# A two-layer hybrid decoder trunk on one core: the opening in a fixed order, the first mixer's order and memory, and the norms' partition sums in two passes

## The chip, the cores and the metric

The kernel runs on 1 core of one Trainium2 chip. Times are microseconds (us) of device time. The times of the kernel before are three runs on one chip. The profile is one further execution, recorded by the hardware profiler.

## What is computed

Two layers over 1024 tokens of width 1024. In each layer the token mixer's width is split into four groups of 256 (short gated convolution, sparse attention, gated linear attention, chunked gMLP) that are fed by one input projection, normalised group by group and joined by one output projection; a squared-ReLU MLP of width 4096 follows. Both halves stand between RMS norms whose scale, shift and gate come from `cond @ w_mod`.

```python
def reference(x, c, ...):
    cond = jax.nn.silu(c)
    for l in range(DEPTH):
        mod = cond @ w_mod[l] + b_mod[l]
        sh1, sc1, gt1, sh2, sc2, gt2 = [m[:, None, :] for m in jnp.split(mod, N_MOD, axis=-1)]
        h = rms_norm(x, norm_g[l, 0]) * (1.0 + sc1) + sh1
        y = mixer_block(h, positions, w_in[l], ..., w_o[l])
        x = x + gt1 * rms_norm(y, norm_g[l, 1])
        h = rms_norm(x, norm_g[l, 2]) * (1.0 + sc2) + sh2
        y = jnp.square(jax.nn.relu(h @ w_up[l])) @ w_down[l]
        x = x + gt2 * rms_norm(y, norm_g[l, 3])
    return x
```

## The kernel before

Activations lie with the width on the partitions: a tile is 128 features by 512 tokens, and `hf` counts the two halves of 512 tokens. The stages are start(), mix(0,0), mix(0,1), ff(0,0), mix(1,0), ff(0,1), mix(1,1), ff(1,0), ff(1,1), where the first number is the layer and the second `hf`. A scheduler reorders the instructions of all stages and gives each engine one stream, which runs in order; the order in which the code is written and priorities (`tc.high_priority`, `LATER`) steer it.

**Matmuls.** Each fp32 operand is split into a high part in fp32r and the rest. `mm3` does a product in three fp32r matmuls (L173 high by high, L174 high by low, L175 low by high). `wunit` brings four 128x128 blocks of weights: a 256 KB load on SyncE's queue (L158), a cast on ScalarE (L167), a subtraction on VectorE (L131). Twelve matmuls belong to a unit, two units to an output tile (`gemm`). Loads go through rings of raw buffers (`raw_a` 3, `raw_b` 3, `raw_f` 5) and split buffers (`w_a` 4, `w_b` 4, `w_f` 6, two per unit). mix(0,0) takes its projection weights through lane "b", its output projection through lane "a"; the MLP takes lane "f".

**Norms.** `rms_R` squares eight (or two) tiles on ScalarE, adds them on VectorE, sums over partitions by one fp32 matmul with a matrix of ones (L195) and takes the inverse root by a logarithm and an exponential (L199, L200). 33 norms are done: 31 over 512 tokens, 2 (the last) over 256. `make_h` scales and shifts the tiles and splits them into `h` (L140, L209).

**Modulation.** A column of `w_mod` is summed against `cond` by a VectorE instruction with an accumulator: in start() 1024 wide (`mod_dot`, L239, tiles `mw`), later in two halves of 512 (`mod_half`, L247), whose 256 KB loads go through `raw_b` in mix(0,0) and through `raw_f` in the MLPs.

**start().** It builds the rotary tables, reads x and six blocks of `w_in` (`EARLY`), does the columns of shift and scale one k at a time, and makes `h` k by k; with each k go 18 matmuls into six PSUM banks, 144 in all. The scheduler orders all of it. x of half 1 is loaded behind it.

**mix(0,0).** Gates, attention (`nsa_part`; its steps transpose probabilities, cast and subtract them, and multiply them with the values: L777, L779, L782, L783), GLA (`gla_part`, a loop over four chunk pairs that starts at L592), gMLP and convolution, then the 24 columns of gate 1, shift 2 and scale 2 in 48 halves (`mods_now`), the attention's group norm, the split of all eight group tiles, and the output projection (`yo`, L946). `between` does the first norm of half 1 there.

**Ends of the mixers.** After the output projection come a norm, the residual with a reload of x (`xo`) and a second norm (`h2`); `LATER` lowers their priority by 800 in all mixers but the first. ff(1,0)'s last down-projection group adds into tiles `yf` of a region of its own.

## Time and profile before

| | us |
|---|---|
| median of 3 runs (lowest, highest) | 2635.78 (2635.64, 2638.55) |
| the profiled execution | 2634.88 |
| its span | 2633.1 |
| TensorE (PE) busy | 2488.4 (95%) |
| VectorE (DVE) busy | 1631.0 (62%) |
| ScalarE (ACT) busy | 1310.5 (50%) |
| mean DMA rate | 116 GB/s |

Busy time of a matmul overlaps that of the next one, so the distance from one start to the next is what a matmul costs in a full stream. In a list of waits a row names the waiting engine, the tile that it writes and its line, then what it waited for, with the time in total, the number of waits and the longest. In the time order each row has start, duration, engine, line, operation, output and inputs, shape and count (rows of neighbours of one kind are joined); in brackets stands the idle time ahead of it on its engine and what ended it.

### The profile page before, as it was taken

What the parts mean: (1) busy time and instruction counts of PE and PEld (TensorE: products, weight loads), DVE (VectorE), ACT (ScalarE), POOL (GpSimd) and SP (SyncE); (2) the same over time, 40 slices, a digit from 0 to 9 for tenths busy, and PEclk for the clock granted to TensorE, in tenths of its full rate; (3) what the DMA queues carried; (4) which work ended last, traced back from release to release, by engine and by line L of the source; (5) the groups of instructions that cost most, each with busy time, mean ns of one, the idle gap of its engine ahead of it and who ended that gap; (6) DMA issues with size and microseconds to landing.
All of it is one profiled execution on the core that took longest, in us unless ns stands there. A gap on an engine that the chain in (4) does not pass through costs nothing.

```text
span 2633.1 us, 34406 instructions
## 1 busy us (share of the span) xinstructions
PE 2488.4 (95%) x11834; PEld 1987.3 (75%) x11834; DVE 1631.0 (62%) x3425; ACT 1310.5 (50%) x2657; POOL 53.0 (2%) x65
## 2 busy tenths in 40 slices
PE   5899499999999999999999999999999998899997
PEld 3666277777877878887787878877788876788886
DVE  7676866557888577444676476544567755634445
ACT  3573345445665356344366445444466744443333
POOL 0100000000000000000100000000100000000000
PEclk9899699999999999999999999999999999999999
DMA  8313634345434454322522344322322134433332
GB/s 279 100 46 100 203 117 132 106 140 153 129 123 134 155 164 140 102 85 89 154 83 70 116 152 140 99 84 79 119 77 68 57 108 143 136 97 96 97 97 75
DMA packets 176200, 305.79 MB, mean 116 GB/s; under 512 B 21573, under 2 KB 33434, under 8 KB 176026
## 3 DMA queue, kind: packets, MB, share of 16 engines
q1 hardware_dynamic: 176026, 303.60, 36.7%
q8 instruction: 93, 1.52, 0.2%
q14 instruction: 81, 0.66, 0.1%
HBM read 281.50 MB, written 17.83 MB: 114 GB/s over the span
## 4 chain that ended last, share of the span: by engine, by line
PE 83%; DVE 6%; DMA 4%; issue 1%; ACT 1%; POOL 0%; DVEq 0%; SPq 0%; ACTq 0%; POOLq 0%
PE ps_ff L173 16%; PE ps_ff L174 16%; PE ps_ff L175 16%; PE ps_mm L173 8%; PE ps_mm L175 8%; PE ps_mm L174 8%; DMA raw_f<-in_w_mod_dram 2%; PE ps_pv L783 1%; PE ps_mm L777 1%; PE ps_pv L782 1%; PE ps_s L822 1%; DMA raw_b<-in_w_mod_dram 1%; PE ps_s L824 1%; PE ps_t L777 1%; PE ps_t L195 1%
## 5 line engine op out<-in xcount | busy, mean ns | idle before, releaser
L167 ACT CAST w_f<-raw_f 128x512 fp32r<-128x512 f32 x504 | 311.7, 619 | 426.3 <-PE ps_ff L174 409.2
L131 DVE TENSOR_TENSOR w_f<-raw_f,w_f 128x512 fp32r<-128x512 f32 x504 | 350.4, 696 | 178.7 <-ACT w_f L167 167.9
L173 PE MATMUL ps_ff<-hid,w_f 128*128 128x512 f32 x992 | 395.4, 399 | 21.7 <-DVE yf L137 12.7
L175 PE MATMUL ps_ff<-h,w_f 128*128 128x512 f32 x1024 | 405.4, 396 | 1.2 <-DVE w_f L131 1.2
L173 PE MATMUL ps_ff<-h,w_f 128*128 128x512 f32 x1024 | 403.1, 394 | 0.0
L174 PE MATMUL ps_ff<-h,w_f 128*128 128x512 f32 x1024 | 402.3, 393 | 0.0
L174 PE MATMUL ps_ff<-hid,w_f 128*128 128x512 f32 x992 | 392.4, 396 | 1.5 <-DVE hid L131 1.5
L175 PE MATMUL ps_ff<-hid,w_f 128*128 128x512 f32 x992 | 391.7, 395 | 0.0
L173 PE MATMUL ps_mm<-h,w_a 128*128 128x512 f32 x784 | 318.2, 406 | 32.6 <-ACT yo L946 23.7
L175 PE MATMUL ps_mm<-h,w_a 128*128 128x512 f32 x784 | 317.2, 405 | 6.0 <-DVE w_a L131 6.0
L174 PE MATMUL ps_mm<-h,w_a 128*128 128x512 f32 x784 | 314.8, 403 | 3.6 <-DVE h L131 3.6
L167 ACT CAST w_a<-raw_a 128x512 fp32r<-128x512 f32 x196 | 121.3, 620 | 304.5 <-PE ps_mm L174 278.7
L131 DVE TENSOR_TENSOR w_a<-raw_a,w_a 128x512 fp32r<-128x512 f32 x196 | 135.1, 689 | 179.2 <-ACT w_a L167 173.3
L173 PEld LDWEIGHTS ps_ff<-hid,w_f 128*128 128x128 f32 x992 | 188.1, 190 | 69.8 <-DVE yf L137 15.2
L175 PEld LDWEIGHTS ps_ff<-h,w_f 128*128 128x128 f32 x1024 | 192.3, 188 | 45.5 <-issue 2.9
L173 PEld LDWEIGHTS ps_ff<-h,w_f 128*128 128x128 f32 x1024 | 192.4, 188 | 43.0 <-issue 3.1
L174 PEld LDWEIGHTS ps_ff<-h,w_f 128*128 128x128 f32 x1024 | 192.4, 188 | 42.0 <-issue 2.2
L174 PEld LDWEIGHTS ps_ff<-hid,w_f 128*128 128x128 f32 x992 | 188.3, 190 | 44.6 <-issue 2.9
L175 PEld LDWEIGHTS ps_ff<-hid,w_f 128*128 128x128 f32 x992 | 187.9, 189 | 41.1 <-issue 1.4
L137 DVE TENSOR_TENSOR y<-y,ps_ff 128x512 f32<-128x512 f32 (+1 forms) x208 | 138.0, 664 | 125.0 <-PE ps_ff L175 123.8
L173 PEld LDWEIGHTS ps_mm<-h,w_a 128*128 128x128 f32 x784 | 149.9, 191 | 72.8 <-ACT yo L946 24.1
L175 PEld LDWEIGHTS ps_mm<-h,w_a 128*128 128x128 f32 x784 | 149.8, 191 | 44.5 <-DVE w_a L131 7.7
(390 smaller groups left out, 3610.2 us busy)
## 6 DMA issues: line engine op xcount, KB each, us to landing
raw_f<-in_w_up_dram SPq DMA_DIRECT2D x256, 256.0 KB, 2.7
raw_f<-in_w_down_dram SPq DMA_DIRECT2D x256, 256.0 KB, 2.7
raw_a<-in_w_in_dram SPq DMA_DIRECT2D x132, 256.0 KB, 2.6
raw_f<-in_w_mod_dram SPq DMA_DIRECT2D x112, 256.0 KB, 2.9
raw_a<-in_w_o_dram SPq DMA_DIRECT2D x64, 256.0 KB, 2.7
raw_b<-in_w_mod_dram SPq DMA_DIRECT2D x48, 256.0 KB, 3.1
mw<-in_w_mod_dram SPq DMA_DIRECT2D x16, 512.0 KB, 5.7
bp<-in_cmp_w_dram SPq DMA_DIRECT2D x32, 256.0 KB, 5.7
```

The source lines that it names most:

```text
L131: V.tensor_tensor(out=out, in0=a, in1=b, op=ALU.subtract)
L137: eng.tensor_tensor(out=out, in0=a, in1=b, op=ALU.add)
L167: A.copy(hi, raw)
L173: PE.matmul(ps_ap, wh, xh, start=start, stop=False)
L174: PE.matmul(ps_ap, wh, xl, start=False, stop=False)
L175: PE.matmul(ps_ap, wl, xh, start=False, stop=stop)
L195: PE.matmul(p, ones, acc, start=True, stop=True)
L777: PE.transpose(tp[0:kn, hh, :], cols(h0 + hh), ident)
L782: PE.matmul(pv[:, h0:h0 + nh, :], vst, th[0:kn], start=first[0], stop=False)
L783: PE.matmul(pv[:, h0:h0 + nh, :], vst, tl[0:kn], start=False, stop=last)
L822: PE.matmul(sp[:, 0:w], qh[:, h0 + hh, :], KX[:, 128 * k0:128 * k0 + w], start=True, stop=False)
L824: PE.matmul(sp[:, 0:w], ql[:, h0 + hh, :], KX[:, 128 * k0:128 * k0 + w], start=False, stop=True)
```

## The change

Three things are changed, and two small ones with them.

1. start() is written in a fixed order (`tc.manual_schedule()`). The small loads (gains, biases, frequencies, positions, selection matrix) and the stores of the rotary tables go to GpSimd's queue. The order of the large loads is c, x, the first two `mw`, six weight blocks, four `mw`, and so on, with six `mw` tiles instead of four. The rotary tables are a generator whose pieces stand between the k steps. `h` is made by a VectorE multiplication with R, a ScalarE scaling and shift, and `split` (ScalarE cast, VectorE subtraction). x of half 1 is loaded in `between`.
2. In mix(0,0) a generator, `beside["b"]`, does one of the 24 modulation columns behind each lane-"b" weight unit until all are done. The attention's group norm is written right behind attention; groups are split one by one; all regions of memory are open at once, with GLA's tiles in the ring of x tiles ("y", 8) and in the pool of `h`. The output projection does the second half of the width (GLA and attention) of six outputs into six PSUM banks first, then the first half, then two whole outputs.
3. In `rms_R` the accumulated squares are cast to fp32r on ScalarE, the rest is taken on VectorE, and two fp32r matmuls with ones replace the fp32 one.
4. `LATER` of mix(1,1) is 0 instead of 800.
5. In ff(1,0) `yf` and `xo` lie in the pool of `h` (`spare`).

```diff
-LATER = {(0, 0): 0, (0, 1): 800, (1, 0): 800, (1, 1): 800}
+LATER = {(0, 0): 0, (0, 1): 800, (1, 0): 800, (1, 1): 0}
...
         for n in names:
-            dma(out=par[l][n], in_=src[n][l])
+            P.dma_start(out=par[l][n], in_=src[n][l])
...
             hi, lo = wunit(lane, src[:, 4 * kh:4 * kh + 4, :], [128, 4, 128])
+            if lane in beside:
+                next(beside[lane], None)
...
+    def gemm_part(ps_ap, lane, src, h, kh, start, stop):
+        hi, lo = wunit(lane, src[:, 4 * kh:4 * kh + 4, :], [128, 4, 128])
+        for k in range(4):
+            mm3(ps_ap, hi[:, k, :], lo[:, k, :], h[4 * kh + k][0], h[4 * kh + k][1],
+                start and k == 0, stop and k == 3)
...
         with tc.high_priority(offset=400):
-            PE.matmul(p, ones, acc, start=True, stop=True)
+            hi, lo = (work.tile([128, T], F32R, name="nt", tag="nt", bufs=3)[:, cs] for _ in range(2))
+            A.copy(hi, acc)
+            sub(lo, acc, hi.bitcast(F32))
+            PE.matmul(p, ones_r, hi, start=True, stop=False)
+            PE.matmul(p, ones_r, lo, start=False, stop=True)
...
+        with region("kw", "right") as kw, region("rp") as rp, region("su") as su, tc.manual_schedule():
...
             for k in range(8):
...
+                msum(k, ms[k])
+                if k == 0:
+                    next(tables)
+                if k < 5:
+                    ms.append(mload(k + 3))
+                if k == 2:
+                    raws = wload(1)
+                mul(xt[k], xt[k], R)
                 if k % 4 == 0:
-                    raws = [wload(n, k // 4) for n in EARLY]
-                hs += make_h(xt, R, d["A1"], d["mod"][:, 0, :], (k,))
...
+                    wsplit(raws)
+                t = nt()
+                A.activation(t, xt[k], AF.Identity, scale=d["A1"][:, k:k + 1], bias=d["mod"][:, 0, k:k + 1])
+                hs.append(split(t))
...
+                next(tables, None)
...
         for j in js:
             for k in range(8):
                 mod_half(l, j, k, lambda src, shape: wraw(lane, src, shape))
-            mod_scale(l, j, slice(0, 8))
+                if k == 7:
+                    mod_scale(l, j, slice(0, 8))
+                yield
...
+                with region("wb", "right") as lane_pool["b"], region("gl", "right") as rg, \
+                        region("cv", "right") as rgc, region("gm", "right") as rgm:
+                    beside["b"] = mods_now(0, (2, 4, 3), "b")
+                    gates, lrT = gate_part(l, hf, h, gr, rg, "a", early)
+                    yn = nsa_part(l, hf, h, es.enter_context(region("ns")), gates, early)
+                    on = [split(t) for t in group_out(yn, "t", gain[:, 2:4])]
+                    ol = [split(t) for t in gla_part(l, hf, h, rg, "b", sx, lrT)]
+                    og = [split(t) for t in gmlp_part(l, hf, h, rgm, "b", sx)]
+                    oc = [split(t) for t in conv_part(l, hf, h, rgc, "b", sx)]
+                    for _ in beside.pop("b"):
+                        pass
...
+            if opening:
+                for o in range(6):
+                    sums[o] = ps(("mm", "mm", "ff", "ff", "s", "s")[o])
+                    gemm_part(sums[o], "a", w_o[l, o], outs, 1, True, False)
             for o in range(8):
-                p = ps("mm")
-                gemm(p, "a", w_o[l, o], outs, (6, 7, 4, 5, 2, 3, 0, 1) if opening else range(8))
+                if o in sums:
+                    p = sums[o]
+                    gemm_part(p, "a", w_o[l, o], outs, 0, False, True)
+                else:
+                    p = ps("mm")
+                    gemm(p, "a", w_o[l, o], outs, range(8))
...
-            down(NGRP - 1, yo=lambda: rg.tile([128, T], F32, name="yf", tag="yf", bufs=8))
+            down(NGRP - 1, yo=(lambda: rg.tile([128, T], F32, name="yf", tag="yf", bufs=8)) if l == 0 else spare)
...
-    xt = load_x(1)
-    h = mix(0, 0, h, lambda: norm(0, 1, xt), early)
+    h = mix(0, 0, h, lambda: norm(0, 1, load_x(1)), early)
```

Lines move by 2 to 60: L131, L173 to L175, L195, L239, L247, L777, L782 and L592 of before are L133, L177 to L179, L210 with L211, L255, L263, L827, L832 and L642 of after.

VectorE in the opening, before, in the middle of the k steps. `ISA mw` is the sum of a 1024-wide column, `ISA ma` its read-out:

```order
L239 ISA mw,ma<-mw,cond 128x1024
L239 ISA ma 128x1
L137 TENSOR_TENSOR mod_100<-ma,bmod_97 128x2
L140 SCALAR_TENSOR_TENSOR nt<-y,A_101,nt 128x512
L239 ISA mw,ma<-mw,cond 128x1024
L239 ISA ma 128x1
L140 SCALAR_TENSOR_TENSOR h<-nt,mod_100,h 128x512
L140 SCALAR_TENSOR_TENSOR A_101<-mod_100,ng_96 128x1
L239 ISA mw,ma<-mw,cond 128x1024
```

The same place after, one k step and the start of the next:

```order
L255 ISA mw,ma<-mw,cond 128x1024
L255 ISA ma 128x1
L255 ISA mw,ma<-mw,cond 128x1024
L255 ISA ma 128x1
L139 TENSOR_TENSOR mod_102<-ma,bmod_99 128x2
L142 SCALAR_TENSOR_TENSOR A_103<-mod_102,ng_98 128x1
L136 TENSOR_TENSOR y<-y,nt 128x512
L133 TENSOR_TENSOR h<-nt,h 128x512
L255 ISA mw,ma<-mw,cond 128x1024
```

The sums of the next columns stood between the two steps of an `h`; now they stand behind its subtraction.

SyncE's queue in the first mixer, before (`raw_b` from w_in is a projection weight, `qh` and `ql` are attention's queries):

```order
L767 DMA qh<-qh 64x2x128 x2
L767 DMA ql<-ql 64x2x128 x2
L158 DMA raw_b<-in_w_in_dram 128x512 x5
L767 DMA qh<-qh 64x2x128 x2
L767 DMA ql<-ql 64x2x128 x2
L158 DMA raw_b<-in_w_in_dram 128x512 x11
```

The same after:

```order
L817 DMA qh<-qh 64x2x128 x2
L817 DMA ql<-ql 64x2x128 x2
L160 DMA raw_b<-in_w_in_dram 128x512
L160 DMA raw_b<-in_w_mod_dram 128x512 x2
L160 DMA raw_b<-in_w_in_dram 128x512
L160 DMA raw_b<-in_w_mod_dram 128x512 x2
L160 DMA raw_b<-in_w_in_dram 128x512
L160 DMA raw_b<-in_w_mod_dram 128x512 x2
```

Weights stood in a row; now two halves of a modulation column stand between any two.

TensorE at the end of attention in the first mixer, before (`ps_mm<-h,w_b` are projections of the mixer):

```order
L175 MATMUL ps_mm<-h,w_b 128x512
L783 MATMUL ps_pv<-w_a,VW 128x512
L777 MATMUL ps_t<-ident,bp 128x128 x4
L455 MATMUL ps_ff<-wsT,xm 64x128 x16
L782 MATMUL ps_pv<-w_a,VW 128x512
L783 MATMUL ps_pv<-w_a,VW 128x512
L777 MATMUL ps_t<-ident,bp 128x128 x4
L173 MATMUL ps_mm<-h,w_b 128x512
```

After, the end of attention, the attention's norm and the start of the GLA loop:

```order
L827 MATMUL ps_t<-ident,bp 128x128 x4
L832 MATMUL ps_pv<-w_a,VW 128x512
L833 MATMUL ps_pv<-w_a,VW 128x512
L827 MATMUL ps_t<-ident,p 32x128 x4
L832 MATMUL ps_pv<-w_a,VC 128x512
L833 MATMUL ps_pv<-w_a,VC 128x512
L210 MATMUL ps_t<-nt,ones_r 128x512
L211 MATMUL ps_t<-nt,ones_r 128x512
L642 MATMUL ps_ff<-gh,g 128x512
L652 MATMUL ps_ff<-gh,g 64x128 x2
```

Projections stood between attention's steps until the end; now none stands between the last twelve steps, the norm and the GLA loop, and the gMLP's and convolution's last 14 units (168 matmuls) stand behind them.

## Rows read from the trace of the kernel before

**Rows 1.** waits of TensorE over the whole run

```profile
PE ps_mm L173 <- ACT yo L946: 23.7, 1, 23.7
...
PE ps_ff L173 <- DVE yf L137: 12.7, 3, 12.1
...
PE ps_mm L173 <- ACT h L222: 7.0, 1, 7.0
...
PE ps_mm L174 <- DVE h L131: 3.6, 1, 3.6
```

**Rows 2.** stretches: length, busy us (count) by engine, granted clock, DMA share, GB/s

```profile
25.00:50.00 25.00, 12.04 (x36) 8.16 (x37) 21.94 (x46) 6.36 (x11) 0.00 (x0) 1.00 0.96 342
...
250.00:275.00 25.00, 10.26 (x32) 5.75 (x30) 21.64 (x60) 9.46 (x17) 0.00 (x0) 0.69 0.64 200
...
275.00:300.00 25.00, 15.47 (x50) 11.29 (x50) 21.57 (x59) 8.39 (x14) 0.64 (x1) 0.77 0.65 203
...
300.00:325.00 25.00, 5.71 (x15) 4.56 (x16) 21.28 (x56) 8.02 (x13) 0.00 (x0) 0.52 0.71 230
```

**Rows 3.** time order of TensorE around a norm's matmul

```profile
292.25 1.02 PE L195 MATMUL ps_t<-nt,ones 128*128 128x512 f32 x2
292.86 0.65 PE L175 MATMUL ps_mm<-h,w_a 128*128 128x512 f32 x1
293.34 0.39 PE L173 MATMUL ps_mm<-h,w_a 128*128 128x512 f32 x1
```

**Rows 4.** group of VectorE up to 82 us; time order of TensorE

```profile
L239 DVE CUSTOM_DVE_ANT_0 mw<-mw,cond 128x1024 f32<-128x1024 f32 x16 | 19.3, 1220 | 1.0 <-DMA mw<-in_w_mod_dram 0.9
...
40.00 1.22 PE L173 MATMUL ps_mm<-h,w_k 128*128 128x512 f32 x2 [11.59 <-ACT h L209]
...
74.76 0.39 PE L175 MATMUL ps_s<-h,w_k 128*128 128x512 f32 x1
...
102.57 0.77 PE L173 MATMUL ps_mm<-h,w_b 128*128 128x512 f32 x1
```

**Rows 5.** SyncE's queue at 108 us; DMA landings; groups of 100:250 and 249:322

```profile
108.25 15.25 SPq L158 DMA_DIRECT2D raw_b<-in_w_in_dram  x5
...
raw_b<-in_w_in_dram SPq DMA_DIRECT2D x11, 256.0 KB, 2.6
...
raw_b<-in_w_mod_dram SPq DMA_DIRECT2D x48, 256.0 KB, 3.1
...
L167 ACT CAST w_b<-raw_b 128x512 fp32r<-128x512 f32 x29 | 17.9, 618 | 24.1 <-PE ps_mm L174 18.6 <-issue 4.4 <-ACT bp L832 1.0
...
L131 DVE TENSOR_TENSOR w_b<-raw_b,w_b 128x512 fp32r<-128x512 f32 x29 | 19.9, 687 | 13.8 <-ACT w_b L167 13.8
...
L247 DVE CUSTOM_DVE_ANT_0 raw_b<-raw_b,cond 128x512 f32<-128x512 f32 x48 | 32.9, 687 | 6.8 <-DMA raw_b<-in_w_mod_dram 6.7
```

**Rows 6.** time order of TensorE, two attention steps

```profile
196.25 0.60 PE L777 MATMUL ps_t<-ident,bp 128*128 128x128 f32 x4
...
198.85 1.05 PE L777 MATMUL ps_t<-ident,bp 128*128 128x128 f32 x4
```

**Rows 7.** time order of TensorE, two starts of the GLA loop

```profile
180.42 1.08 PE L592 MATMUL ps_ff<-g 128*128 128x512 f32 x2
...
185.02 1.08 PE L592 MATMUL ps_ff<-g 128*128 128x512 f32 x2
```

**Rows 8.** time order of TensorE around the output projection's stop

```profile
295.20 0.40 PE L175 MATMUL ps_mm<-h,w_a 128*128 128x512 f32 x1
...
319.29 0.80 PE L173 MATMUL ps_mm<-h,w_a 128*128 128x512 f32 x1 [23.70 <-ACT yo L946]
```

**Rows 9.** time order of TensorE and VectorE at mix(1,1)'s end

```profile
2230.92 2.08 PE L195 MATMUL ps_t<-nt,ones 128*128 128x512 f32 x2 [5.15 <-DVE nt L137]
...
2244.35 1.28 DVE L137 TENSOR_TENSOR yf<-y,ps_ff 128x512 f32<-128x512 f32 x2
...
2245.08 0.79 PE L173 MATMUL ps_ff<-hid,w_f 128*128 128x512 f32 x1 [12.08 <-DVE yf L137]
```

More of the change, by code (lines that the diff above doesn't have):

```diff
@@ L83, in trunk_kernel @@
                     fill=0.0, base=0, channel_multiplier=-1)
+    ones_r = const.tile([128, 128], F32R, name="ones_r")
+    A.copy(ones_r, ones)
     V.memset(bones, 0.0)
@@ L201, in rstd, with make_h @@
         return R
-    def make_h(xt, R, Ac, shc, ks=range(8)):
+    def make_h(xt, R, Ac, shc):
         h = []
-        for k in ks:
+        for k in range(8):
             t = nt()
@@ L266, in start @@
         d = par[0]
-        early = {}
-        rope_tables()
-        with region("kw", "right") as kw, region("su") as su:
-            def mk(src, shape):
-                t = su.tile(shape, F32, name="mw", tag="mw", bufs=4)
-                dma(out=t, in_=src)
-                return t
-            def wload(n, kh):
-                raw = kw.tile([128, 4, 128], F32, name="raw_k", tag="raw_k", bufs=6)
-                dma(out=raw, in_=w_in[0, n, :, 4 * kh:4 * kh + 4, :])
-                return raw
-            def wsplit(raw):
-                hi, lo = (kw.tile([128, 4, 128], F32R, name="w_k", tag="w_k", bufs=12) for _ in range(2))
-                A.copy(hi, raw)
-                sub(lo, raw, hi.bitcast(F32))
-                return hi, lo
+        early, hs, ws = {}, [], {}
@@ new lines, in start, with wload, wsplit, mload @@
+        load_params(0, ("ng", "bmod"))
+        with region("kw", "right") as kw, region("rp") as rp, region("su") as su, tc.manual_schedule():
+            def wload(kh):
+                raws = []
+                for n in EARLY:
+                    raw = kw.tile([128, 4, 128], F32, name="raw_k", tag="raw_k", bufs=6)
+                    dma(out=raw, in_=w_in[0, n, :, 4 * kh:4 * kh + 4, :])
+                    raws.append(raw)
+                return raws
+            def wsplit(raws):
+                for n, raw in zip(EARLY, raws):
+                    hi, lo = (kw.tile([128, 4, 128], F32R, name="w_k", tag="w_k", bufs=12) for _ in range(2))
+                    A.copy(hi, raw)
+                    sub(lo, raw, hi.bitcast(F32))
+                    ws[n] = hi, lo
+            def mload(k):
+                ts = [su.tile([128, 1024], F32, name="mw", tag="mw", bufs=6) for _ in range(2)]
+                for j in (0, 1):
+                    dma(out=ts[j], in_=w_mod[0, 8 * j + k])
+                return ts
+            bm = d["bmod"].rearrange("p (j k) -> p j k", k=8)
+            def msum(k, ts):
+                ma = work.tile([128, 2, 1], F32, name="ma", tag="ma", bufs=4)
+                for j in (0, 1):
+                    mod_dot(0, j, k, lambda src, shape: ts[j], ma[:, j, :])
+                add(d["mod"][:, 0:2, k:k + 1], ma, bm[:, 0:2, k:k + 1])
+                mod_scale(0, 1, slice(k, k + 1))
@@ L286, in start @@
             for hf in range(2):
-                t1, t2 = (su.tile([128, T], F32, name="ct", tag="ct", bufs=4) for _ in range(2))
                 ch = cond[:, hf * T:hf * T + T]
                 dma(out=ch, in_=c[:, hf * T:hf * T + T].to_broadcast([128, T]))
+            xt = load_x(0)
+            tables = rope_tables(rp)
+            for hf in range(2):
+                t1, t2 = otile(), otile()
+                ch = cond[:, hf * T:hf * T + T]
                 logsig(t2, ch, t1)
@@ L337, in trunk_kernel, with rope_tables @@
     sind = dram.tile([2, 128, T], F32, name="sind")
-    def rope_tables():
-        with region("rp") as rp:
+    def rope_tables(rp):
+        if True:
             def tk(n):
@@ L485, in gla_part, with ht @@
         d = par[l]
+        opening = (l, hf) == (0, 0)
         def gt(shape=(128, T)):
+            if opening:
+                return work.tile(list(shape), F32, name="g", tag="y", bufs=8)
             return rg.tile(list(shape), F32, name="g", tag="g", bufs=10)
+        def ht(shape):
+            return hp.tile(list(shape), F32, name="gh", tag="h", bufs=32) if opening else gt(shape)
         def inproj(k):
@@ L935, in mix @@
                 yn = nsa_part(l, hf, h, es.enter_context(region("ns")), gates)
-            on = group_out(yn, "t", gain[:, 2:4])
-            outs = [split(t) for t in oc + og + ol + on]
+                on = group_out(yn, "t", gain[:, 2:4])
+                oc, og, ol, on = ([split(t) for t in g] for g in (oc, og, ol, on))
+            outs = oc + og + ol + on
         res = None
@@ L1054, in load_x @@
             t = ytile()
-            dma(out=t, in_=xT[hf, :, k, :])
+            load(out=t, in_=xT[hf, :, k, :])
             xt.append(t)
```

48 lines of the change are left out of this document (18 added, 30 removed).

## The prediction

> **What bounds the kernel now.** I read the waits of TensorE over the whole run first. The engine is busy 95% of the 2633.1 us span, so some 145 us of idle time are all that an order can win, and a saving elsewhere counts only where TensorE itself is short of time. The waits say where the idle time lies [rows 1]: one of 23.7 us on the copy of an output tile, 7.0 and 3.6 us on the first split tiles of the output projection, and 12.1 us (of 12.7) on the last sums of ff(1,0)'s down projection. The table by stretches puts them on the clock [rows 2]: from 250 to 325 us TensorE works 10.26, 15.47 and 5.71 of 25 us each, 43.6 us lost, at granted clocks of 0.69, 0.77 and 0.52. That is the tail of the first mixer: the 48 modulation columns, two 256 KB loads' worth of VectorE sums each pair, sit in front of the output projection's copies there. Last I read the matmuls of the norms and the stretch in which attention and the gated linear attention (GLA) run.
>
> The profiled run took 2634.88 us (span 2633.1); the median of the runs shown is 2635.78, so a sum made on the trace gets 0.9 added.
>
> **Part 1, the norms' sums.** One fp32 matmul against ones shows as two records that together hold the engine 0.86 us at full clock: the records start at 292.25, the next at 292.86 and the one after at 293.34, of which one ordinary 0.23 us step belongs to the matmul between [rows 3]. Two fp32r passes are two ordinary steps, 0.46. The saving is 0.40 us for each of 31 norms of 512 columns. About 26 lie where TensorE is the bound: 26 x 0.40 = 10.5 us less. Five (opening, mixer's groups, the norm before ff) lie in idle time and save nothing. Each norm also gains a ScalarE cast and a VectorE subtraction before its matmul, 0.62 + 0.69 us by the same operations on a weight unit of equal size [rows 5], so 1.3 us on the chain of a norm that is waited for. Where up-projection matmuls stand behind, that is hidden; in the very last norm nothing stands behind it: +1.1 net. Bounds for this part: -13 (all 31) to -6 (ten of the norms find their matmuls waited for by what follows).
>
> **Part 2, the opening.** Before, VectorE does for each k two sums of 1024 columns (1.22 us each, some 1.15 from start to start) and the two steps of an `h` (an estimated 0.75 each), 3.8 in all, and the first of the 144 early matmuls starts at 40.00, the last starts at 74.76 and is through at 75.3 [rows 4]: from 40 on TensorE sets the pace, 18 matmuls x 0.23 = 4.1 us per k. After, the k step is written in a fixed order: sums, multiply, then ScalarE's scaling and cast, then the subtraction, and the next k's sums stand behind that subtraction on VectorE. Per k: 2.3 + 0.15 + 0.69 + (some 0.7 + 0.62, waited for) + 0.69 + hand-overs, some 5.4 us, now above TensorE's 4.1. The start is earlier, since x and the first w_mod are no longer behind the six weight loads and the second half of x is not loaded here: by my chain (condition ready near 12, eight squares, taken at a cast's 0.62, to 18, first sums 21.6, table operations 4.5, multiply, six weight subtractions x 0.69 [rows 5], subtraction; the 12 and the 4.5 are estimates) the first h is there near 32.5. At k = 4 six weight casts and the table's copy stand in front on ScalarE, and that copy waits for TensorE to finish k = 3: about 5 us more. 32.5 + 7 x 5.4 + 5 + 4.1 = 79.4, against 75.3: +4, between -3 (per k 4.4) and +10 (first h at 38).
>
> **Part 3, the first mixer.** This decides. Gone are the three waits of 23.7, 7.0 and 3.6 us and most of the rest of the 43.6. Three things come instead.
> First, the weight ring. Three raw buffers now take weight, column, column in turn, so each weight has always the same buffer and its load is issued only when the previous weight has been cast and subtracted. Load 2.6 to 3.1, cast 0.62, subtraction 0.69 [rows 5] make 3.9 to 4.4 us; with the two 0.69 us sums and attention's work in VectorE's queue I take 4.5. Before, five weight loads went out in 15.25 us, 3.05 each. TensorE needs 2.75 per unit (12 matmuls). Eighteen units stand before the end of the interleaved part; from a first one near 107 (before 102.57 [rows 4], plus the opening's 4) they last to 107 + 81 = 188, and the attention pieces put among them bring some 6 more: 194.
> Second, with no projection matmul among them, twelve attention steps, the attention's group norm, the GLA loop and its norms now follow one another. A step that runs alone takes 2.6 us, 196.25 to 198.85 [rows 6]; the GLA loop 4.6 per step, 180.42 to 185.02 [rows 7], with other work between. 12 x 2.6 + 9 (norm chain: squares, add, cast, subtraction, logarithm, exponential, two gains, splits) + 4 x 4.6 + 8.5 = 67 (the 9 and the 8.5 are estimates from the durations of such operations), ends 261; before, projections filled this time (29 units are cast between 100 and 250 us [rows 5]).
> Third, fourteen units remain: two stand ready (2.75 each), four still alternate with columns (4.5), eight run at 2.75: 45 us. SyncE's queue has seven loads of the second half of x in the middle of them, 1.8 MB that at 342 GB/s [rows 2] take 5.4 us, with the following weights queued behind; they need the GLA tiles free, which they are by then. Conv ends at 261 + 45 + 5.4 = 311.5, and 16 output units x 2.75 = 44 bring 355; the conv norm hides under the first halves of six outputs (16.5 us), so that no split is waited for. I add 3 for the clock when TensorE comes out of the stretch at half speed, as the granted 0.77 and 0.52 around the restarts show here [rows 2]: 358.
> Before: 295.20 is the last matmul of the second output, and the remaining 144 run from 319.29 [rows 8], 144 x 0.23 + 2 for the low clock, to 354.4. The part is worth +3.5 with the opening in it. Bounds: -10 (attention 2.2, GLA 3.6 per step when VectorE is free, ring 4.2) to +22 (ring 5.5). I stay in the middle because each step has a row.
>
> **Part 4, the end of mix(1,1).** The lowered priority goes, and 60 up-projection matmuls instead of 93 stand behind the residual's norms. Before, the second norm's matmul starts at 2230.92 after 5.15 idle, and the last sums only at 2244.35, in VectorE's queue behind the scaled tiles; TensorE restarts at 2245.08 [rows 9]. After, the norm comes some 5 us earlier and 1.3 later, cover is 33 x 0.23 = 7.6 shorter, but these 33 matmuls still have to be done later: their time is not lost. The sums go to spare tiles, and still stand behind the scaled tiles. I take 0, from -5 to +5.
>
> **Sum.** 2634.88 - 10.5 + 1.1 + 3.5 + 0 = 2629.0, plus 0.9: **2630 us**.
>
> **The rivals.**
> *Ring slower (slower than before).* Each load of a column or weight is waited for in order, and VectorE's queue holds attention's subtractions behind a sum whose load has not landed. At 5.6 us per unit the 18 units cost 18 x 1.1 = 20 us: 2650. It decides from 5.1 per unit on (11 us more than forecast, 2641). For it: the trace before already loses 6.7 us of 73 in VectorE sums waiting for loads [rows 5], and attention's DMAs share the queue. Against: loads are two at a time, with 67 us of slack only afterwards. 0.22.
> *Serial stretch shorter.* If steps alone take 2.2 and GLA 3.6, with VectorE no longer casting weights between, 4.8 + 4 us go, and 3 more in the norms: 2618. 0.18.
> *Opening at half clock.* TensorE would work 4.1 of every 5.4 us. In 275 to 300 it worked 15.47 of 25 and was granted 0.77 [rows 2]; at the low level of the two (1.2 against 2.4 GHz) the 0.23 us step becomes up to 0.46, so 18 take up to 8.2 us, more than VectorE's 5.4. Eight of those, 66, from 32.5 end at 98, 19 later than forecast: 2649. Against it: from 25 to 50 us the engine was busy 12.04 of 25 and was granted 1.00 [rows 2]. 0.06. The Trainium skill (TensorE: Matmul & The Clock Gate, HAM oscillation) has a kernel whose bursts of matmuls between waits fell back to the half rate every time; by it this rival would be the forecast.
> *Norms win nothing.* If what follows a norm waits for its longer chain, the 10.5 go: 2640. 0.08.
>
> **How the numbers follow.** The forecast has 0.46, with a range of its own of 2618 to 2641. About 0.2% (5.3 us) is what a measurement of this kernel tells from no change: 2630.5 to 2641.1. Of the forecast's 0.46, 0.27 lies below that and 0.19 in it. Faster: 0.27 + 0.18 = 0.45; same: 0.19 + 0.08 = 0.27; slower: 0.22 + 0.06 = 0.28. The range reaches from the shorter stretch's lower side, 2610, to a little past the ring's 2650: 2653.
>
> **What will show it.** The first early matmul near 32 us and the last near 79; weight loads of the first mixer 4.5 us apart; between about 194 and 261 us no projection matmul and a granted clock near half; no wait of 20 us on an output copy; the output projection done near 358; the norm's two matmuls 0.46 us together. It is wrong if projections start again before 250 or after 275, or if the time up to the second mixer moves by over 15 us.

## The result, and the profile after

| | before | after |
|---|---|---|
| median, us (lowest, highest) | 2635.71 (2633.18, 2638.55) | 2681.78 (2677.83, 2684.12) |
| span of the profiled execution | 2633.1 | 2682.1 |
| TensorE idle, summed over its waits | 133.1 | 164.3 |

The ratio is 1.0173 [1.0155, 1.0191]: the change makes the kernel 46 us slower. The forecast was 2630, and the upper end of its range 2653.

The two spans are 49 us apart. Where these come from is read by putting the same matmul of both traces side by side, counted from the start of its kind:

| matmul | before | after | shift |
|---|---|---|---|
| first of the 144 early ones | 40.00 | 29.75 | -10.2 |
| last of the 144 | 74.76 | 100.55 | +25.8 |
| first with lane "b" weights (`w_b`) | 102.57 | 133.09 | +30.5 |
| last of the 18th unit | 207.94 | 211.22 | +3.3 |
| last with `w_b` | 255.76 | 357.11 | +101 |
| last of the output projection | 355.22 | 401.82 | +46.6 |
| second norm behind the first mixer (L195, L210) | 388.49 | 435.85 | +47.4 |
| last norm in front of mix(1,1)'s end | 1872.14 | 1914.04 | +41.9 |
| end of the span | 2633.1 | 2682.1 | +49.0 |

So nearly everything is lost in the first 402 us: 26 us in the opening, partly regained by units that go early, then far more in the first mixer.

TensorE's waits over the whole run (in total, times, longest), against [rows 1]: the largest are now on norms and on the `h` of the opening, and none is on an output tile `yo`. The 18.4 us are the time ahead of TensorE's first instruction.

```profile
PE ps_t L210 <- ACT nt L208: 36.2, 4, 18.4
...
PE ps_mm L177 <- ACT h L238: 25.9, 8, 9.8
```

**The opening.** TensorE's rows of after, in order of time, are these. Line L177 is `mm3`'s first matmul (L173 before), L417 the transposes of the table's piece, L423 its selection:

```profile
29.75 0.80 PE L177 MATMUL ps_mm<-h,w_k 128*128 128x512 f32 x1 [9.85 <-ACT h L238]
...
41.67 0.49 PE L177 MATMUL ps_mm<-h,w_k 128*128 128x512 f32 x1 [2.03 <-ACT h L238]
...
46.48 1.12 PE L423 MATMUL ps_pv<-nt,sl 17*128 17x512 f32 x2
49.63 0.49 PE L177 MATMUL ps_mm<-h,w_k 128*128 128x512 f32 x1 [2.04 <-ACT h L238]
...
80.05 0.79 PE L177 MATMUL ps_mm<-h,w_k 128*128 128x512 f32 x1 [2.04 <-ACT h L238]
...
87.21 1.12 PE L423 MATMUL ps_pv<-nt,sl 17*128 17x512 f32 x2
...
90.37 0.50 PE L177 MATMUL ps_mm<-h,w_k 128*128 128x512 f32 x1 [2.04 <-ACT h L238]
```

The k steps start 8.0 us apart (41.67, 49.63) and 10.3 us apart later (80.05, 90.37). The later one is longer because its 18 matmuls take 7.2 us (80.05 to 87.21), where the granted clock is 0.60 (80.00 to 87.30), against 4.8 us (41.67 to 46.48) at 1.00 (41.60 to 46.50). ScalarE's rows at the same place:

```profile
39.68 0.57 ACT L419 COPY nt<-ps_t 17x512 f32<-17x512 f32 x1 [9.98 <-PE ps_t L417]
40.16 0.81 ACT L343 ACTIVATE nt<-y,mod,A 128x512 f32<-128x512 f32 x1
41.00 0.62 ACT L238 CAST h<-nt 128x512 fp32r<-128x512 f32 x1
47.63 0.59 ACT L425 COPY of<-ps_pv 128x512 f32<-128x512 f32 x1 [6.02 <-PE ps_pv L423]
```

ScalarE sits idle for 9.98 and 6.02 us in front of a copy whose matmul stands behind all 18 of step k. Behind that copy in its queue stand the scaling and the cast that make `h` of step k+1. So TensorE cannot start k+1 until it has ended k, its own table piece, a copy, a scaling and a cast: at full clock that is 4.8 us from 41.67 to 46.48 (18 x 0.23 and the wait for the low half of `h`) and 3.2 from there to 49.63. Six of the seven steps have such a copy.

**The first mixer.** Windows of after (start:end, its length, busy time and count of PE, PEld, DVE, ACT and POOL, granted clock, DMA share, GB/s), to be held against [rows 2]:

```profile
25.00:50.00 25.00, 14.03 (x43) 9.53 (x43) 14.64 (x38) 5.25 (x8) 0.57 (x1) 1.00 0.44 143
50.00:75.00 25.00, 17.36 (x54) 12.16 (x54) 15.03 (x30) 6.94 (x12) 0.54 (x1) 0.81 0.42 150
75.00:100.00 25.00, 19.75 (x63) 13.11 (x62) 9.73 (x22) 6.87 (x11) 1.49 (x3) 0.85 0.37 126
...
225.00:250.00 25.00, 17.98 (x47) 10.36 (x47) 8.85 (x23) 6.72 (x18) 0.00 (x0) 0.50 0.10 37
250.00:275.00 25.00, 12.67 (x30) 5.57 (x30) 11.07 (x28) 7.93 (x17) 1.27 (x2) 0.50 0.12 38
275.00:300.00 25.00, 17.65 (x56) 9.37 (x56) 4.75 (x18) 6.79 (x18) 1.90 (x3) 0.50 0.10 32
300.00:325.00 25.00, 16.73 (x83) 13.21 (x84) 17.64 (x33) 10.81 (x21) 0.00 (x0) 0.71 0.26 85
```

From 225 to 300 the count of matmuls is small, VectorE, ScalarE and GpSimd are idle most of the time, DMA moves 32 to 38 GB/s, and the clock is at its lower level throughout. TensorE's rows of that stretch show what runs there: attention steps (L827), the attention's norm (L210), the GLA loop (L642), and the first projection at the end:

```profile
211.22 0.40 PE L179 MATMUL ps_mm<-h,w_b 128*128 128x512 f32 x1
...
212.85 0.60 PE L827 MATMUL ps_t<-ident,bp 128*128 128x128 f32 x4
...
239.20 1.05 PE L827 MATMUL ps_t<-ident,bp 128*128 128x128 f32 x4
...
242.24 1.05 PE L827 MATMUL ps_t<-ident,bp 128*128 128x128 f32 x4
...
259.33 0.79 PE L210 MATMUL ps_t<-nt,ones_r 128*128 128x512 f32 x1 [4.73 <-ACT nt L208]
...
266.06 2.04 PE L642 MATMUL ps_ff<-gh,g 128*128 128x512 f32 x2 [5.21 <-DVE gh L638]
...
272.96 2.02 PE L642 MATMUL ps_ff<-gh,g 128*128 128x512 f32 x2
...
279.84 2.02 PE L642 MATMUL ps_ff<-gh,g 128*128 128x512 f32 x2
...
309.20 0.78 PE L177 MATMUL ps_mm<-h,w_b 128*128 128x512 f32 x1
```

No projection matmul runs from 211.22 to 309.20, 98 us. Yet two units were split and ready long before 309: VectorE's last subtractions for `w_b` lie at 213.58 and 220.18, and the next projection matmul stands in TensorE's stream behind the whole chain.

```profile
213.58 0.69 DVE L133 TENSOR_TENSOR w_b<-raw_b,w_b 128x512 fp32r<-128x512 f32 x1
...
220.18 0.69 DVE L133 TENSOR_TENSOR w_b<-raw_b,w_b 128x512 fp32r<-128x512 f32 x1
```

The loads of the weights in the interleaved part are issued 5.30 us apart here, with two halves of a column behind each; over all 18 units the pace is (211.22 - 133.09) / 18 = 4.34 us.

```profile
203.56 0.33 SPq L160 DMA_DIRECT2D raw_b<-in_w_in_dram  x1
204.17 1.85 SPq L160 DMA_DIRECT2D raw_b<-in_w_mod_dram  x2
208.86 0.33 SPq L160 DMA_DIRECT2D raw_b<-in_w_in_dram  x1
```

TensorE hardly waits for them. The window of the 18 units (columns as above), and all of TensorE's waits in it, 1.5 us together:

```profile
133.00:211.30 78.30, 76.70 (x413) 60.82 (x412) 65.39 (x217) 49.21 (x129) 0.00 (x0) 0.95 0.52 159
...
PE ps_pv L833 <- DVE w_a L133: 1.2, 1, 1.2
PE ps_mm L179 <- DVE w_b L133: 0.3, 1, 0.3
```

**The norms, and the end of mix(1,1).** Two norm matmuls of after (L210, L211) stand among projections, each 0.23 from the next start, against [rows 3]:

```profile
326.81 0.39 PE L210 MATMUL ps_ff<-nt,ones_r 128*128 128x512 f32 x1
327.04 0.40 PE L177 MATMUL ps_mm<-h,w_b 128*128 128x512 f32 x1
...
327.51 0.39 PE L211 MATMUL ps_ff<-nt,ones_r 128*128 128x512 f32 x1
327.74 0.40 PE L179 MATMUL ps_mm<-h,w_b 128*128 128x512 f32 x1
```

At the end of mix(1,1) the waits of TensorE, against [rows 9], are 10.64 and 13.63 where they were 5.15 and 12.08:

```profile
2277.38 0.80 PE L210 MATMUL ps_t<-nt,ones_r 128*128 128x512 f32 x1 [10.64 <-ACT nt L208]
2292.53 0.80 PE L177 MATMUL ps_ff<-hid,w_f 128*128 128x512 f32 x1 [13.63 <-DVE sp L139]
```

### The profile page after: what moved, and what is told of

It is laid out like the page before. It is cut to its first block, busy times and chain, and to the rows that moved or that the text cites. A ratio compares the mean times of both kernels' runs of the same rounds, so it can differ in the third digit from the quotient of the medians.

```text
span 2682.1 us, 34487 instructions
## 1 busy us (share of the span) xinstructions
PE 2506.1 (93%) x11834; PEld 1997.6 (74%) x11834; DVE 1652.6 (62%) x3458; ACT 1337.3 (50%) x2699; POOL 63.5 (2%) x80
## 4 chain that ended last, share of the span: by engine, by line
PE 81%; DVE 9%; DMA 5%; ACT 2%; issue 2%; SPq 0%; POOL 0%; DVEq 0%; POOLq 0%; ACTq 0%
PE ps_ff L177 16%; PE ps_ff L178 16%; PE ps_ff L179 16%; PE ps_mm L178 7%; PE ps_mm L177 7%; PE ps_mm L179 7%; DMA raw_f<-in_w_mod_dram 2%; DMA raw_b<-in_w_mod_dram 1%; PE ps_pv L833 1%; PE ps_pv L832 1%; PE ps_mm L827 1%; PE ps_t L827 1%; PE ps_s L872 1%; PE ps_s L874 1%; DMA bp<-in_cmp_w_dram 1%
## 5 line engine op out<-in xcount | busy, mean ns | idle before, releaser
L133 DVE TENSOR_TENSOR w_f<-raw_f,w_f 128x512 fp32r<-128x512 f32 x504 | 348.3, 692 | 212.9 <-ACT w_f L169 177.4
L177 PE MATMUL ps_ff<-hid,w_f 128*128 128x512 f32 x992 | 395.6, 399 | 20.8 <-DVE sp L139 13.6
L179 PE MATMUL ps_ff<-h,w_f 128*128 128x512 f32 x1024 | 402.7, 394 | 0.3
L177 PE MATMUL ps_ff<-h,w_f 128*128 128x512 f32 x1024 | 401.7, 392 | 0.5 <-ACT r L1043 0.5
L179 PE MATMUL ps_ff<-hid,w_f 128*128 128x512 f32 x992 | 392.6, 396 | 0.0
L177 PE MATMUL ps_mm<-h,w_a 128*128 128x512 f32 x752 | 300.7, 400 | 3.3 <-ACT nt L200 2.1
L179 PE MATMUL ps_mm<-h,w_a 128*128 128x512 f32 x752 | 299.3, 398 | 1.8 <-DVE w_a L133 1.7
L178 PE MATMUL ps_mm<-h,w_a 128*128 128x512 f32 x752 | 299.5, 398 | 0.0
L177 PEld LDWEIGHTS ps_ff<-hid,w_f 128*128 128x128 f32 x992 | 188.2, 190 | 67.6 <-DVE sp L139 14.1
L133 DVE TENSOR_TENSOR w_a<-raw_a,w_a 128x512 fp32r<-128x512 f32 x196 | 134.9, 688 | 167.4 <-ACT w_a L169 157.3
L179 PEld LDWEIGHTS ps_ff<-h,w_f 128*128 128x128 f32 x1024 | 192.3, 188 | 43.1 <-DVE w_f L133 1.6
L177 PEld LDWEIGHTS ps_ff<-h,w_f 128*128 128x128 f32 x1024 | 192.3, 188 | 42.6 <-issue 1.4
L179 PEld LDWEIGHTS ps_ff<-hid,w_f 128*128 128x128 f32 x992 | 188.6, 190 | 41.8 <-issue 1.3
L179 PEld LDWEIGHTS ps_mm<-h,w_a 128*128 128x128 f32 x752 | 142.2, 189 | 37.7 <-DVE w_a L133 3.5
L177 PEld LDWEIGHTS ps_mm<-h,w_a 128*128 128x128 f32 x752 | 142.0, 189 | 37.4 <-ACT nt L200 2.5
```

Of the source, the lines that this page charges most:

```text
L133: V.tensor_tensor(out=out, in0=a, in1=b, op=ALU.subtract)
L177: PE.matmul(ps_ap, wh, xh, start=start, stop=False)
L178: PE.matmul(ps_ap, wh, xl, start=False, stop=False)
L179: PE.matmul(ps_ap, wl, xh, start=False, stop=stop)
```

## The experiments

Each ratio is to the kernel before, run on the same chip, with its 95% interval.

**The opening: where the table pieces stand.** My theory after the first look: the ScalarE copies ahead of the next scaling cost the opening its 26 us. `tables_behind` puts all pieces behind the eight steps, `tables_ahead` puts each ahead of the step's 18 matmuls, `start_as_before` takes the whole opening of before.

```diff
 # tables_ahead
                 hs.append(split(t))
+                if k:
+                    next(tables, None)
                 for i, n in enumerate(EARLY):
...
-                next(tables, None)
 # tables_behind
-                next(tables, None)
+            for _ in tables:
+                pass
```

> The changed kernel with the six later pieces of the rotary tables (TensorE, ScalarE copies, stores) put behind the eight k steps instead of between them. Theory T (a table piece stands behind the 18 matmuls of step k on TensorE, and its copy ahead of the scaling of step k+1 on ScalarE, so that TensorE waits for an h that waits for TensorE): steps of 5.4 us instead of 8 to 10, the last early matmul near 78 instead of 100.6, and 18 to 22 us less than the changed kernel, 2660 to 2664. Rival (the opening's delay is absorbed in the first mixer, which waits for its weights anyhow, or VectorE's order sets the step): 2675 or more, or steps that stay above 7 us.

> The changed kernel with each later table piece put ahead of the 18 matmuls of its step instead of behind them; its ScalarE copy then waits for the matmuls of the step before only. Theory T: steps of 5.4 us, last early matmul at 76 to 80, tables ready at about k = 6, so that the first projection of the mixer comes at 102 to 108 instead of 133; 24 to 30 us off the changed kernel: 2652 to 2658. Rival (the pieces themselves cost the time wherever they stand, or the step stays TensorE's at the low clock): early matmuls end above 88, 2665 or more.

> The changed kernel with start(), the tables and the small loads of before; the first mixer, norms and the rest as changed. Theory T: the first projection of the mixer starts at 102 to 105 instead of 133, and 26 to 30 us go: 2652 to 2656, still 16 to 20 above before. Rival (delay absorbed): 2672 or more.

| | us | ratio | last early matmul | first `w_b` |
|---|---|---|---|---|
| after | 2681.78 | 1.0173 | 100.55 | 133.1 |
| tables_behind | 2671.3 | 1.0136 [1.0121, 1.0152] | 76.6 | 123.5 |
| tables_ahead | 2659.63 | 1.0094 [1.0080, 1.0108] | 77.45 | 110.1 |
| start_as_before | 2658.65 | 1.0086 [1.0073, 1.0100] | 76.66 | 109.6 |

ScalarE's rows of `tables_ahead` show the scalings 5.57 us apart, waiting for VectorE and no longer for TensorE (but for the one behind the six weight casts of k = 4):

```profile
41.24 0.82 ACT L343 ACTIVATE nt<-y,mod,A 128x512 f32<-128x512 f32 x1 [1.82 <-DVE y L136]
...
44.02 0.59 ACT L426 COPY of<-ps_pv 128x512 f32<-128x512 f32 x1 [1.32 <-PE ps_pv L424]
46.81 0.82 ACT L343 ACTIVATE nt<-y,mod,A 128x512 f32<-128x512 f32 x1 [2.20 <-DVE y L136]
```

The theory stands: the same work with the pieces moved ahead of the matmuls is 22 us faster, about as much as going back to the old opening (23). All three came out above their forecasts, `tables_ahead` and `start_as_before` by 2 and 3 us, `tables_behind` by 7. `tables_behind` repairs the 144 matmuls just as well and gains only 10.5, because the tables are then on the way to attention: from the last early matmul to the first `w_b` it takes 47 us, against 33 in `tables_ahead`. Both `start_as_before` and `tables_ahead` keep the first `w_b` some 7 us later than before; that belongs to the first mixer's new order, and I did not follow it further.

**The first mixer: what holds the GLA loop back.** `mixer_as_before` takes mix(0,0) of before with the new opening.

> The changed kernel with the first mixer's order, memory and output projection of before (columns behind the convolution, projections among attention's steps, whole outputs); opening, norms and the rest as changed. Theory M (the serial stretch from attention's end to the GLA norms costs more than the stop of 23.7 us that it replaced): the opening's 26 stays, the mixer's 16 goes, 2662 to 2668. Rival (the new mixer is itself a gain and all the loss is the opening's): 2690 to 2705.

It gives 2661.29, 1.0100 [1.0084, 1.0117]: the new mixer costs 20.5 us, net of what it saves. GLA's loop has its own matmuls and projections that need nothing of attention. In after its three tiles (`gh`) come out of the ring of `h`, which attention's probabilities (`bp`) use too, and their clearing waits for attention's transposes:

```profile
218.60 1.45 POOL L634 MEMSET gh<- 128x512 f32 x3 [103.62 <-PE ps_t L827]
```

`gh_early` takes and clears the three tiles ahead of attention, from the same ring, and leaves everything else.

```diff
+                    ghs.extend(hp.tile([128, T], F32, name="gh", tag="h", bufs=32) for _ in range(3))
+                    for buf in ghs:
+                        P.memset(buf, 0.0)
                     gates, lrT = gate_part(l, hf, h, gr, rg, "a", early)
```

> The changed kernel with the three GLA tiles that share the ring of h taken and cleared ahead of attention instead of behind it, so that they do not wait for attention's last probabilities, which come from the same ring. Theory G (that shared ring holds the GLA loop back behind attention; 4 steps of 6.9 us and a wait of 5 then stand in the serial stretch): loop among attention's steps again, the stretch from the last projection to the next 25 to 35 us shorter, 2650 to 2660. Rival (the loop's work only moves and lengthens the part before): 2672 or more.

It gives 2650.52, 1.0058 [1.0044, 1.0071]: 31 us less than after. Its first GLA step stands among projections at full clock, and the stretch without projections is 222.73 to 281.24, 58.5 us instead of 98:

```profile
175.69 0.39 PE L836 MATMUL ps_pv<-w_a,VW 128*128 128x512 f32 x1
175.92 1.02 PE L646 MATMUL ps_ff<-gh,g 128*128 128x512 f32 x2
```

So the tile ring is the largest single cause of the loss. It works through the order: in after the clearing stands at 218.60, 47 us ahead of the loop's first matmul at 266.06, so what costs the time is not that wait itself but the place behind attention that the loop was given in every engine's stream when its tiles came free late.

**The modulation columns.** `columns_behind` keeps the new order and memory and does the 24 columns behind the convolution, as before.

```diff
-                    beside["b"] = mods_now(0, (2, 4, 3), "b")
...
                     oc = [split(t) for t in conv_part(l, hf, h, rgc, "b", sx)]
-                    for _ in beside.pop("b"):
+                    for _ in mods_now(0, (2, 4, 3), "b"):
```

> The changed kernel with the 24 columns behind the convolution, nothing else. Ring rival of the prediction (the ring costs the time): 2660 or less. Theory now (opening 23, GLA loop behind attention some 30; the ring runs at the forecast 4.3 us and is no cause): 2675 to 2695, since the serial stretch stays.

It gives 2694.88, 1.0227 [1.0213, 1.0241], 13 us more than after, and the wait on an output copy is back (`yo`, in 350 to 460 us):

```profile
PE ps_mm L177 <- ACT yo L1007: 22.1, 1, 22.1
```

Spreading the columns is thus worth 13 us here, with a stop of 22 removed; where the other 9 go was not traced. The ring is not where they go: without columns in it the first 18 units take 75.2 us (128.19 to 203.40), 4.18 each, hardly less than the 4.34 of after.

**The end of mix(1,1).** `late_as_before` has `LATER` at 800 and the region of before for `yf` and `xo`.

> The changed kernel with LATER of mix(1,1) at 800 again and ff(1,0)'s last sums and reload in their region again; all else as changed. Theory L (parts 4 and 5 cost the 6 us by which the changed kernel falls back further at the boundary of mix(1,1) and ff(1,0), where the kernel with the norms alone loses 1): 2675 to 2678, TensorE's idle time there 20 to 24 instead of 28. Rival (the loss there comes from the norms' longer chain, and parts 4 and 5 do nothing): 2680 to 2683.

It gives 2673.39, 1.0153 [1.0139, 1.0167], 8.4 less than after by the medians; the two intervals overlap. The number in `LATER` does nothing: with everything else as in after, the order on all five engines is the same with 0 and with 800. So what there is comes from the memory. The two profiled spans are 10.7 us apart (2682.1 and 2671.4). Of these 5.6 were there at the norm at 1914.04 already (1908.44 here), where the two kernels are alike, so that much differs from run to run; the other 5 come behind it. The waits there are 11.01 and 12.08:

```profile
2270.64 0.79 PE L210 MATMUL ps_t<-nt,ones_r 128*128 128x512 f32 x1 [11.01 <-ACT nt L208]
2284.24 0.80 PE L177 MATMUL ps_ff<-hid,w_f 128*128 128x512 f32 x1 [12.08 <-DVE yf L139]
```

The long first wait is not the memory's either: `norms_chosen` (below), which has the priority, the memory and these two norms of before, has it too.

```profile
2226.55 2.08 PE L200 MATMUL ps_t<-nt,ones 128*128 128x512 f32 x2 [9.53 <-DVE nt L139]
...
2240.71 0.80 PE L175 MATMUL ps_ff<-hid,w_f 128*128 128x512 f32 x1 [12.09 <-DVE yf L139]
```

**The norms.** `norms_only` is before with two passes in every norm; `norms_chosen` has them except where a norm is waited for (opening, first mixer, the residual norms of mix(1,1), the last norm in ff(1,1)); `norms_exposed` has them only there; `after_chosen` is after with the choice of `norms_chosen`. The edit of `norms_chosen` (`norms_exposed` asks `if two[0]`):

```diff
         p = ps(pt)[:, cs]
+            if not two[0]:
+                PE.matmul(p, ones, acc, start=True, stop=True)
+                return rstd(p, inv_n, mk()[:, cs])
```

> The kernel before with the norms' two passes alone. Theory N (the two passes save TensorE 0.40 us for each of some 26 norms that it bounds, as forecast): 2627 us, 8 to 10 below before, the two records of a norm 0.23 us apart. Rival (the longer chain of cast and subtraction is waited for and eats it): 2632 to 2640, with waits of TensorE for the norm's cast or subtraction of 5 us and more in sum beside those of before.

> The kernel before with the two passes only in norms that are not waited for: not in start(), the first mixer, the residual norms of mix(1,1) and the last norm. Theory N2 (the two passes win 8 to 9 us where TensorE is the bound, as between 385 and 1877 us of the run with all norms, and lose 11 us in the first mixer and some 2 later, where the chain is waited for): 2625 to 2629. Rival (re-ordering, not the chain, made the differences): anything from 2632 up.

> The kernel before with the two passes only in the norms that are waited for (start(), first mixer with the first norm of half 1, residual norms of mix(1,1), last norm); the fp32 pass in all others. If the loss of the run with all norms (6.3 us above before) is the exposed norms' and the rest's gain is the 7.4 of the run with the chosen ones, this is 12 to 15 us above before: 2648 to 2651. Rival (the loss came from elsewhere, such as re-ordering in the middle stages): within 5 us of before.

> The changed kernel with the two passes only in norms that are not waited for. Theory N2 (a waited-for norm pays for cast, subtraction and two passes at the low clock): 6 to 13 us less than the changed kernel, 2669 to 2676. Rival (inside the changed kernel's order the exposed norms cost nothing more): 2679 to 2683.

| | us | ratio | against before, us |
|---|---|---|---|
| norms_only | 2642.18 | 1.0026 [1.0016, 1.0036] | +6.3 |
| norms_chosen | 2628.63 | 0.9977 [0.9968, 0.9986] | -7.4 |
| norms_exposed | 2649.82 | 1.0050 [1.0037, 1.0064] | +12.6 |
| after_chosen | 2681.24 | 1.0171 [1.0156, 1.0185] | (after: no difference) |

-7.4 and +12.6 make 5.2, near the +6.3 of all norms, which lies above both of that run's forecasts (2627; 2632 to 2640). In `norms_only` the second norm behind the first mixer is 11.9 us later than in before (400.41 against 388.49), the last one in front of mix(1,1)'s end 3.5 (1875.68 against 1872.14): over the covered norms the shift falls by 8.4. `after_chosen` was forecast at 2669 to 2676 by the same theory and failed it: inside after the exposed norms cost nothing that shows. TensorE's waits for norm tiles in 255 to 300 us, where before has 4.9 and 4.4 (9.3 in all), are 14.1 together:

```profile
PE ps_ff L200 <- ACT nt L198: 5.6, 1, 5.6
PE ps_t L200 <- ACT nt L198: 5.1, 1, 5.1
...
PE ps_t L201 <- DVE nt L133: 2.4, 1, 2.4
PE ps_ff L201 <- DVE nt L133: 1.0, 1, 1.0
```

That is 4.8 of the 11.9. The other 7 are not shown by a run of their own. The order of the first mixer's instructions differs there (the longest stretch without projections is 28.2 us, in before 22.3, and in `norms_chosen` 22.2), so I put them down to the scheduler's other choices; which of the moved instructions costs them stays open.

**All repairs together.** `combined` has `tables_ahead`, `gh_early`, the late memory of before and the chosen norms. `combined_cols` has the columns behind the convolution besides; `combined_two` has two passes in every norm.

> The changed kernel with four things at once: table pieces ahead of the matmuls of their step, the three GLA tiles taken ahead of attention, yf and xo of ff(1,0) in their region (with LATER 800), and the two passes only in norms that are not waited for. If the causes are separate, their gains add up: 22 + 31 + 8 from 2681.8 make 2620, and the chosen norms take up to 10 more: 2610 to 2620, below the kernel before. Rival (they share cover: with the table and the GLA loop out of the way the first mixer is bound by its weight ring): 2630 or more.

> The same with the 24 modulation columns behind the convolution instead of beside the weight units. Theory R (the ring weight, column, column sets the pace of the first 18 units, 4.3 us each, and costs more than the columns in the tail): units 3.1 us apart and 5 to 15 us less than the run with columns beside. Rival (the columns stand in front of the output projection again, as in the kernel before, and its stop comes back): 5 to 25 us more.

> The combined kernel (2625) with the two passes in all norms instead of the chosen ones. If exposed norms cost as in the kernel before, 8 to 14 us more: 2633 to 2639. If they cost nothing, as inside the changed kernel's own order (2681.2 with chosen against 2681.8 with all), 2623 to 2627.

| | us | ratio |
|---|---|---|
| combined | 2625.07 | 0.9959 [0.9945, 0.9972] |
| combined_cols | 2631.32 | 0.9982 [0.9973, 0.9992] |
| combined_two | 2627.46 | 0.9966 [0.9953, 0.9978] |

`combined` is faster than both kernels, by 11 and 57 us. Its forecast was 2610 to 2620 if the gains add up, and 2630 or more if they share cover: it came between the two. Its output projection ends at 349.5, where before has 355.2, and its gap without projections is 198.11 to 257.42, still 59 us. `combined_cols` loses 6 of that, where 5 to 15 less had been forecast if the ring set the pace, and has a 20.4 us wait on `yo` again. In `combined_two` the exposed norms cost 2.4 us, which the intervals do not tell from nothing: the 12.6 of `norms_exposed` are not a fixed price of the longer chain but depend on the order around it.

## Why the prediction was wrong

**Part 2 failed at one step: "At k = 4 six weight casts and the table's copy stand in front on ScalarE, and that copy waits for TensorE to finish k = 3."** The mechanism is right and was counted once. ScalarE's order has such a copy at six of seven steps. The 5.4 us per k would have held without it (5.57 in `tables_ahead`, with the last early matmul at 77.45 against 79 forecast), and the first matmul even came at 29.75 instead of 32.5. With the copies the seven steps from 29.75 to 96.02 take 9.5 us each. That is +26 on the first `w_b` (133 against 107), and `tables_ahead` against after puts 22 us of the total on it. Some 6 of the 26 came with the clock: the 18 matmuls from 57.59, 69.66 and 80.05 took 6.3, 7.2 and 7.2 us at granted clocks of 0.73, 0.59 and 0.60, where 4.8 are enough at 1.00. So the rival "Opening at half clock" came in part, in the steps that the copies had stretched.

**Part 3, first step: the size was near, by luck; the mechanism was wrong.** The 18 units took 78 us instead of 87, 4.34 each where the ring was to give 4.5, and the rival "Ring slower" (5.6) did not come. But the ring does not set this pace. TensorE waits for 1.5 of the 78 us, and `columns_behind`, with weights alone in the ring, takes 4.18 each. TensorE's own work sets it: counted from start to start, the 216 projection matmuls take 54 us (the first of them at the lower clock) and the matmuls among them 24, some 19 of these attention's, for which the forecast had 6. The row of before was misread as well: five loads in 15.25 us have four gaps between their starts, 3.7 us each and not 3.05.

**Part 3, second step: this is the other half.** The stretch was forecast at 67 us and took 98:

| | forecast | measured |
|---|---|---|
| attention to its last product (211.2 to 254.6) | 31.2 | 43.4 |
| norm (to 266.1) | 9 | 11.5 |
| GLA loop (to 294) | 18.4 | 27.9 |
| its norms and gMLP transposes (to 309.2) | 8.5 | 15.2 |

Two things were wrong in it. The durations came from [rows 6], a step that ran alone but at a granted clock of 0.82 (196.25 to 198.85), and from [rows 7], where the clock was 1.00 and attention's products ran between, while the forecast itself said that the clock would be near half. At the lower level (0.50, 1.2 of 2.4 GHz) the attention step is 3.04 us (239.20 to 242.24) instead of 2.6, the GLA step 6.88 (272.96 to 279.84) instead of 4.6, with its first pair of matmuls at 2.02 instead of 1.08. And GLA's place behind attention was taken from the order without asking for its cause. The forecast said that the loop follows attention; that its tiles wait for a shared ring, which could be had otherwise, was not seen, and so neither that the price depends on it. `gh_early` shows 31 us for it. The Trainium skill (TensorE: Matmul & The Clock Gate, HAM oscillation) describes a kernel whose bursts of matmuls, each shorter than the DMA wait behind it, went back to the half rate every time. The stretch is at the half rate too (0.50 from 225 to 300), though its attention steps hold one wait of 0.68 us in 3.04; the opening was only in part (1.00, 0.81 and 0.85). How much of the 31 us the clock alone takes was not separated: no run here had the same order at the other level. The rows at either level are all there is on it.

**Part 3, third step: right in the main.** From 309.2 to the last `w_b` it takes 47.9 us (forecast 50.4), and 44.7 more to the end of the output projection (forecast 44, and 3 for the clock). There is no wait on `yo`. The 5.4 us for the second half of x were not paid: its loads went out from 291.49 on, ahead of these units. The terms add up to the miss: +26 for the opening, -9 for the units, +31 for the stretch, -4 for the rest make 44, and the output projection ended at 401.8 instead of 358.

**Part 1: the size of a norm was right, the sentence "Five (opening, mixer's groups, the norm before ff) lie in idle time and save nothing" was not.** Two passes are 0.46 us as forecast. 21 norms are covered, not 26, and 21 x 0.40 is 8.4: they bring 7 to 8 us where they stand alone (-7.4 in `norms_chosen`, and the fall of 8.4 in `norms_only`). In before's order the 12 exposed ones cost 12.6; I had priced them at nothing, but for 1.1 at the last. The rival "Norms win nothing" had this wait, and its 2640 was near the 2642.18 of `norms_only`. In after itself the shift between the same two norms falls by only 5.5 (47.4 to 41.9); the 3 us between that and 8.4 were not traced.

**Part 4: 0 was forecast; from the norm at 1872.14 to the end the shift grows by 7.1, in `late_as_before` by 2.0.** So, by one profile of each, some 5 us belong to the memory of `yf` and `xo`, at the bound of the range; the later wait (13.63 against 12.08) holds 1.5 of them, and the rest was not traced. The shorter cover came, but not from `LATER`: 60 up-projection and down-projection matmuls stand between the last `w_a` of mix(1,1) and the second norm in after, in `late_as_before`, in `norms_only` and in `norms_chosen`, and 93 in before and in `norms_exposed`. So it comes with the two passes in the covered norms. The wait is longer by it (10.64, 11.01, 9.98 and 9.53 against 5.15), but the other 33 matmuls, 7.6 us, are done earlier: as forecast, their time is not lost.

The two criteria of the prediction's last part both told it was wrong: projections began again at 309, not before 275, and the time up to the second mixer moved by 46.6 us.

## What to carry to other kernels

When small work is put between the steps of a pipelined loop, look at where its copy out of PSUM stands in the copying engine's queue: behind the next step's producer it is free, ahead of it the two engines take turns, at 4 us a step here. When tiles are moved to a shared ring to save memory, ask of each new tenant whose release it now waits for; a loop that needed nothing of attention was tied to its end by three tiles. Before a ring of buffers is taken for the pace of a stretch, count TensorE's own work in it: here that alone filled the time. And durations for a stretch that will run alone must be read from rows that ran alone at the clock that the forecast gives it.

## What the runs showed of the hardware that I had not expected

- The granted clock stayed at 0.50 from 225 to 300 us although PE is listed as busy for 72%, 51% and 71% of the three windows: transposes and short products with hand-overs between them. Identical steps there take 1.05 us (four transposes) and 2.02 us (two GLA matmuls), against 0.60 for the same four transposes at 212.85 and 1.02 for two GLA matmuls in `gh_early`, where the clock was 1.00.
- Weights that were ready at 221 us were first used at 309: TensorE's stream is in order, and no loaded weight helped what stood behind the chain in it. The Trainium skill (PSUM — Partial Sum Buffer, Engine vs sequencer instructions) says that matmuls start and complete in program order; the trace agrees.
- The same lengthening of the exposed norms' chains (a cast and a subtraction) cost 12.6 us in one order of the surrounding instructions (`norms_exposed`) and 2.4 or nothing in others (`combined_two`, `after_chosen`).
